# Second column parts of a feed-forward unit that stream one more tile of columns in their matmuls

## The chip, the core and the metric

The kernel runs on one NeuronCore of one Trainium2 chip. The metric is the device time of one execution in microseconds; the time before is the median of three runs. The profile is one further execution, recorded by the hardware profiler, with a time of its own.

## The reference

One decoder layer for a prompt of 2048 positions and a group of 8 x 4 sample positions that share the weights: RMSNorm, one input projection, dilated attention and a gated unit, output projection, then a SwiGLU feed-forward part, a residual add and a final RMSNorm. All in float32. The part that the change touches is the feed-forward:

```python
def _swiglu(x, g, w_gate, w_up, w_down):
    h = _rmsnorm(x, g)
    return (jax.nn.silu(h @ w_gate) * (h @ w_up)) @ w_down
# D_MODEL = 1024, D_FF = 2816
```

## The kernel before

The first thousand microseconds hold the projections and the attention; the rest is output projection and feed-forward, which go through the prompt in three blocks: `Block(0, 6)`, `Block(6, 12)` and `Block(12, NT)`, tiles of 128 rows. Blocks 0 and 1 have six tiles, the last one four, plus the sample rows, whose columns are dealt out to its tiles.

The two products with w_gate and w_up are computed together by a scheme of seven products instead of eight (Strassen's, in Winograd's form) over halves of the rows and of the inner dimension. So the feed-forward runs in units: one unit is one of the 22 columns of 128 hidden features (`f`), for all tiles of a block, in seven products `q = 0..6`. `product` (L1651) makes one of them: four slices of the inner dimension, and for each three matmuls (L1661 to L1663), since every float32 operand is split into a high and a low part in the faster format fp32r, and high x high, high x low and low x high are summed in PSUM. That is 12 matmuls a product, 84 a unit. The weight part (`op`, 128x128 slices) is the stationary operand; the block's normalised input (`xh2`, `xl2`, made by `Operands`, L1464) is the moving one, with a width of `B.w` columns for each tile: 64 in blocks 0 and 1, 68 in the last one. A whole unit streams 6 x 64 = 384 or 4 x 68 = 272 columns in each matmul.

`ps_m` (L87) hands out four PSUM banks in turn. After the matmuls ACT copies the first product out (L1671), DVE adds the others up (L1673 to L1690), ACT applies silu (L1701), and `hidden` (L1704) multiplies and splits the result into `hw`, high part by ACT (L1711), low part by DVE one step later (through `later` and `tick`, L1316 to L1324). Every second unit, `down_unit` (L1719, matmuls L1734) multiplies two units' results by w_down, in two halves for each tile, into two PSUM banks in turn, and DVE adds them to `acc` (L1736).

The stationary operands of unit f + 1 are prepared while unit f runs (`prepare`, L1625, from `one`, L1991): ACT rounds (`high`, L1600), GpSimd subtracts (`low_half`, L1604). In block 0 they are also made there from the weights for the first time, ACT scaling them by the norm's gain (L1572) and GpSimd forming the scheme's four sums (`sums`, L1584 to L1593), and are then stored to `ab_d`; blocks 1 and 2 load them from there. The rows of w_down are split by ACT and GpSimd as well (`split_down`, L1647, by `split_sb` at L135 and L138). Each engine works through its instructions in the order in which the program issues them, written out by hand.

The first unit of each block (f = 0) is cut in two column parts, so that it can begin while the last tiles' operands are still being made: `part = 4 if B.nt == 6 else 2`, and

```python
units = [dict(f=0, a=0, b=part), dict(f=0, a=part, b=B.nt)] + [dict(f=f, a=0, b=B.nt) for f in range(1, NF)]
```

So in blocks 0 and 1 the first part streams tiles 0 to 3 (256 columns) and the second one tiles 4 and 5 (128 columns); in the last block both stream two tiles (136 columns). During the second part the operands of unit 1 are prepared (L2002), as beside any other unit.

Of the kernel before, what the change touches and what calls it, by code (L numbers as in the profile page):

```python
# [65 lines left out]
def hymba_step(ctx: ExitStack, tc: tile.TileContext, A: dict, O: dict):  # L66
# [20 lines left out]
    def ps_m(which=None):  # L87

        if which is None:
            turn[3] = which = (turn[3] + 1) % 4  # L90
        return pool_["pm"].tile([P, 512], F32, name="ps_m%d" % which, tag="m%d" % which, bufs=1)
# [610 lines left out]
    for half in range(2):  # L702
        for ki, kind in enumerate(ORDER[half]):
            for gi, tiles in enumerate(GROUPS):
                start = ((half * 5 + ki) * 3 + gi) * 8
                for k in range(KD):
                    if start == 0:

                        for j in range(3):
                            n = 3 * k + j  # L710
# [7 lines left out]
                for j, tj in enumerate(tiles):  # L718
# [7 lines left out]
                    ps = lambda key=key, j=j: outs[key][j]  # L726
# [459 lines left out]
    def weights_of(d, steps, n0=0, n1=NT):  # L1186
        w = {}
        at(*steps[0], lambda: w.update(w=Weights(d["s"], n0, n1)))
        for (y, ph), fn in zip(steps, "weights_a weights_b weights_c weights_d weights_e turn store".split()):
            at(y, ph, lambda fn=fn: getattr(w["w"], fn)())  # L1190
        return w

    def steps_of(s0, *steps):
        return [(s0 + y, ph) for y, ph in steps]

    last_half = {}
    for h in range(H):
# [4 lines left out]
        if end:  # L1202

            x = s0 - NI
            d = stats_of(h, dve, steps_of(x, (11, "misc"), (13, "early"), (14, "early")))
            w = weights_of(d, steps_of(x, (14, "misc"), (15, "early"), *[(15, "misc")] * 3), 0, NT // 2)
# [24 lines left out]
    for i, it in enumerate(items):  # L1231
        x, h, n = B0 + i, it["h"], it["n"]
# [47 lines left out]
    TOK = (0, 4, 1, 3, 5, 2, 6)  # L1280
# [9 lines left out]
    def wide_pair(name):  # L1290

        t_ = rp.tile([P, 2, 1024], F32R, name=name, tag="wide", bufs=2)
        return t_[:, 0], t_[:, 1]
# [22 lines left out]
    def later(n, fn, *args, ahead=False):  # L1316
        due[clock[0] + n, not ahead, len(seq)] = (fn, args)
        seq.append(0)
# [332 lines left out]
    def product(B, u, q):  # L1651

        f, a, b = u["f"], u["a"], u["b"]
        n = (b - a) * B.w
        ps = ps_m()[:, 0:n]
        wh, wl = ops[f, q]
        xh, xl = (x[:, a:b, TOK[q]] for x in B.ops)
        out = ps.rearrange("p (i w) -> p i w", w=B.w)
        for k in range(4):
            ks = slice(k * P, (k + 1) * P)  # L1660
            pe.matmul(out, wh[:, ks], xh[:, :, k], start=(k == 0), stop=False)  # L1661
            pe.matmul(out, wh[:, ks], xl[:, :, k], start=False, stop=False)  # L1662
            pe.matmul(out, wl[:, ks], xh[:, :, k], start=False, stop=(k == 3))  # L1663

        rings = ((raw_tile, raw_tile, raw_tile, zn_tile), (zn_tile, zn_tile, zn_tile, raw_tile), (zn_tile, raw_tile, zn_tile, raw_tile))[min(u["n"], 2)]
        if q in (0, 1, 3, 4):
            v = (0, 1, None, 2, 3)[q]
            u["t", v] = rings[v]()[:, 0:n]
        c11, c21, c12, c22 = (u.get(("t", v)) for v in range(4))
        if q == 0:  # L1670
            act.activation(c11, ps, AF.Copy)  # L1671
        elif q == 1:
            dve.tensor_add(c21, c11, ps)  # L1673
        elif q == 2:
            dve.tensor_add(c11, c11, ps)
            u["g", 0] = silu_of(u, 0, c11)
        elif q == 3:
            dve.tensor_add(c12, c21, ps)
            u["s1"] = ps
        elif q == 4:  # L1680
            dve.tensor_add(c21, c21, ps)
            dve.tensor_add(c22, c21, u["s1"])  # L1682
        elif q == 5:
            dve.tensor_add(c12, c12, ps)  # L1684
            u["g", 1] = silu_of(u, 1, c12)
        elif q == 6:
            if a == 0:
                B.h[f % FC] = wide_pair("hw") + (hs4[:, f // FC % 2 * FC + f % FC] if B.last else None,)
            lows = hidden(B, u, 1, c22)
            dve.tensor_add(c21, c21, ps)  # L1690
            lows += hidden(B, u, 0, c21)
            for args in lows:
                if f + 1 < NF:
                    later(1, dve.tensor_sub, *args)
                else:
                    dve.tensor_sub(*args)

    def silu_of(u, z, c):

        g = bank(z)[:, 0:c.shape[-1]] if u["f"] else c  # L1700
        act.activation(g, c, AF.Silu)  # L1701
        return g

    def hidden(B, u, zz, c):  # L1704

        f, a, b, g = u["f"], u["a"], u["b"], u["g", zz]
        dve.tensor_mul(g, g, c)  # L1707
        hh, hl, hs_ = B.h[f % FC]
        g = g.rearrange("p (i w) -> p i w", w=B.w)
        hi, lo_ = (v[:, a * P:b * P].rearrange("p (i z c) -> p i z c", z=2, c=64)[:, :, zz] for v in (hh, hl))  # L1710
        act.activation(hi, g[:, :, 0:64], AF.Copy)  # L1711
        lows = [(lo_, g[:, :, 0:64], hi.bitcast(F32))]
        if B.last:
            hi, lo_ = (hs_[:, v * SR:(v + 1) * SR].rearrange("p (z i c) -> p z i c", z=2, i=B.nt)[:, zz, a:b] for v in range(2))
            act.activation(hi, g[:, :, 64:], AF.Copy)
            lows.append((lo_, g[:, :, 64:], hi.bitcast(F32)))
        return lows
# [66 lines left out]
    B = blocks[0]  # L1784
# [192 lines left out]
    for bi, B in enumerate(blocks):  # L1977
# [13 lines left out]
        def one(u, q):  # L1991
            tick()
            product(B, u, q)
            f = u["f"]
            if u["b"] < B.nt:
# [173 lines left out]
```

## Time and profile before

| what | value |
|---|---|
| median of 3 runs | 2611.22 us (2607.18 to 2616.19) |
| the profiled execution: its own time | 2606.15 us |
| its span, first to last instruction | 2604.4 us |
| mean granted TensorE clock | 0.979 |
| TensorE, matmuls | 2484.0 us busy, 95% |
| DVE, ACT, GpSimd | 54%, 47%, 53% busy |
| matmuls of `product`, lines L1661 to L1663 | 3 x 1932, 618 us each line |
| matmuls of `down_unit`, line L1734 | 2040 of 128x512, 484 us |

How to read it: a group's line has the source line, the engine and operation, out<-in by the program's names, the shape (128x384 is partitions x streamed columns) and the count; then busy time and the mean duration of one in ns; then the idle time of the engine just before them, and who ended it. Matmuls are pipelined: the duration of one is longer than the distance from one start to the next, so costs are read from distances of starts. PE is TensorE, POOL is GpSimd; the granted clock is a share of full speed.

### The profile page before, as it was taken

The numbers are of one execution on the slowest core, as the hardware profiler recorded it, in microseconds if no ns is written. First come the engines' busy times: TensorE is split into PE (matmuls) and PEld (weight loads), VectorE is DVE, ScalarE is ACT, GpSimd is POOL, SyncE is SP. The second block draws the span as 40 slices with busy tenths as digits, with TensorE's granted clock in tenths as the row PEclk, the third lists the DMA queues.
The fourth block names the chain that finished last, engine by engine and source line by source line (L and its number), as shares of the span: only waits on it lengthen the run. The fifth ranks groups of instructions, "written<-read, shape, count | busy, mean of one in ns | idle before, by whom it ended". The sixth has DMA issues, their size and how long they took to land. (4 is left out here: it accounts for less than half of the span.)

```text
span 2604.4 us, 38948 instructions
## 1 busy us (share of the span) xinstructions
PE 2484.0 (95%) x13598; PEld 2192.0 (84%) x13598; DVE 1411.0 (54%) x2772; ACT 1220.7 (47%) x2567; POOL 1373.8 (53%) x1074
## 2 busy tenths in 40 slices
PE   8998899999999889999999999999999999999997
PEld 6777687677988777988989988999999987999996
DVE  3359686345888856444444465444444466444445
ACT  6423334446877746554554545332323335444332
POOL 2035754123576656775766743563544534666663
PEclk9999999999999999999999999999999998999998
DMA  7764853578687664464553564464554643555553
GB/s 244 223 204 146 279 152 126 180 249 271 185 231 222 170 191 159 154 201 143 177 183 129 195 184 144 170 208 156 174 186 147 209 156 118 206 197 199 198 196 110
DMA packets 313408, 479.99 MB, mean 184 GB/s; under 512 B 25841, under 2 KB 178834, under 8 KB 307326
## 3 DMA queue, kind: packets, MB, share of 16 engines
q1 hardware_dynamic: 307740, 468.48, 55.9%
q10 hardware_dynamic: 5474, 9.04, 1.2%
q8 instruction: 108, 1.77, 0.3%
q14 instruction: 86, 0.70, 0.1%
HBM read 381.72 MB, written 165.83 MB: 210 GB/s over the span
## 5 line engine op out<-in xcount | busy, mean ns | idle before, releaser
L1604 POOL TENSOR_TENSOR op<-fr,op 128x512 fp32r<-128x512 f32 x385 | 488.7, 1299 | 299.1 <-ACT op L1600 279.1
L1661 PE MATMUL ps_m<-xh,op 128*128 128x384 f32 (+4 forms) x1932 | 618.6, 320 | 3.7 <-DVE zn L1682 3.7
L1663 PE MATMUL ps_m<-xh,op 128*128 128x384 f32 (+4 forms) x1932 | 618.1, 320 | 0.0
L1662 PE MATMUL ps_m<-xl,op 128*128 128x384 f32 (+4 forms) x1932 | 617.2, 319 | 0.0
L1734 PE MATMUL ps_o<-dw,hw 128*128 128x512 f32 x2040 | 484.0, 392 | 13.1 <-DVE acc L1736 13.1
L1734 PEld LDWEIGHTS ps_o<-dw,hw 128*128 128x128 f32 x2040 | 379.6, 188 | 95.9 <-DVE acc L1736 19.8
L1661 PEld LDWEIGHTS ps_m<-xh,op 128*128 128x128 f32 x1932 | 371.8, 192 | 8.3 <-issue 2.7
L1662 PEld LDWEIGHTS ps_m<-xl,op 128*128 128x128 f32 x1932 | 371.6, 192 | 3.5
L1663 PEld LDWEIGHTS ps_m<-xh,op 128*128 128x128 f32 x1932 | 371.6, 192 | 0.0
L1736 DVE TENSOR_TENSOR acc<-acc,ps_o 128x512 f32<-128x512 f32 (+1 forms) x362 | 247.1, 687 | 213.7 <-PE ps_o L1734 213.7
L1701 ACT ACTIVATE ps_t<-zn 128x384 f32<-128x384 f32 (+1 forms) x126 | 58.3, 463 | 474.0 <-DVE zn L1684 367.8
L1600 ACT ACTIVATE op<-fr 128x512 fp32r<-128x512 f32 x396 | 235.3, 623 | 22.2 <-DMA fr<-ab_d 14.9
L138 POOL TENSOR_TENSOR dw<-fd,dw 128x1024 fp32r<-128x1024 f32 x66 | 158.7, 2405 | 122.1 <-ACT dw L135 122.1
L318 PE MATMUL ps_s<-wh,xh 128*128 128x512 f32 x480 | 197.9, 412 | 6.5 <-ACT xh L135 5.9
L319 PE MATMUL ps_s<-wl,xh 128*128 128x512 f32 x480 | 192.4, 401 | 1.0 <-DVE wl L226 1.0
L320 PE MATMUL ps_s<-wh,xl 128*128 128x512 f32 x480 | 191.6, 399 | 0.0
L1604 POOL TENSOR_TENSOR op<-pair,op 128x512 fp32r<-128x512 f32 x63 | 81.5, 1302 | 117.1 <-ACT op L1600 117.1
L1711 ACT ACTIVATE hw<-ps_t 128x384 fp32r<-128x384 f32 (+1 forms) x126 | 56.0, 453 | 175.3 <-DVE ps_t L1707 174.4
L318 PEld LDWEIGHTS ps_s<-wh,xh 128*128 128x128 f32 x480 | 93.0, 194 | 36.4 <-issue 8.3
L320 PEld LDWEIGHTS ps_s<-wh,xl 128*128 128x128 f32 x480 | 92.8, 193 | 20.6 <-DVE xl L138 0.3
L319 PEld LDWEIGHTS ps_s<-wl,xh 128*128 128x128 f32 x480 | 93.1, 194 | 19.7 <-DVE wl L226 2.2
L611 POOL TENSOR_TENSOR vl<-kv,vh 100x512 fp32r<-100x512 f32 (+1 forms) x32 | 46.0, 1438 | 109.9 <-ACT vh L605 43.9
(484 smaller groups left out, 4776.1 us busy)
## 6 DMA issues: line engine op xcount, KB each, us to landing
fr<-ab_d SPq DMA_DIRECT2D x308, 256.0 KB
fd<-in_w_down_dram SPq DMA_DIRECT2D x66, 512.0 KB
out_ks_dram<-in_cache_k_dram SPq DMA_DIRECT2D x56, 512.0 KB
out_vs_dram<-in_cache_v_dram SPq DMA_DIRECT2D x56, 512.0 KB
ab_d<-fr SPq DMA_DIRECT2D x88, 256.0 KB
raw<-in_w_in_dram SPq DMA_DIRECT2D x72, 256.0 KB
qk_d<-pair SPq DMA_DIRECT2D x64, 256.0 KB
ab_d<-pair SPq DMA_DIRECT2D x63, 256.0 KB
```

The lines of the kernel that those rows point to most:

```text
L138: (eng_lo or pool).tensor_sub(lo, src, hi.bitcast(F32))
L318: pe.matmul(o[j], xh[:, k, :], wh, start=(k == 0), stop=False)
L319: pe.matmul(o[j], xh[:, k, :], wl, start=False, stop=False)
L320: pe.matmul(o[j], xl[:, k, :], wh, start=False, stop=(k == KD - 1))
L1600: act.activation(ops[f, j][0], ab[f][j], AF.Copy)
L1604: (pool if f or j in POOL_LOW else dve).tensor_sub(lo_, ab[f][j], hi.bitcast(F32))
L1661: pe.matmul(out, wh[:, ks], xh[:, :, k], start=(k == 0), stop=False)
L1662: pe.matmul(out, wh[:, ks], xl[:, :, k], start=False, stop=False)
L1663: pe.matmul(out, wl[:, ks], xh[:, :, k], start=False, stop=(k == 3))
L1701: act.activation(g, c, AF.Silu)
L1734: pe.matmul(ps[0:nr], l_, r_[:, cs], start=(z == 0 and y == 0), stop=(z == FC - 1 and y == len(pairs) - 1))
L1736: dve.tensor_add(B.acc[i][0:nr, cs], B.acc[i][0:nr, cs], ps[0:nr])
```

## The change

In `product`, a part that doesn't begin at tile 0 takes the tile in front of it along: `lead` is 1 for the second part of a block's first unit, and 0 for all other units. The matmuls' moving operand starts one tile earlier and their output is wider by `B.w` columns: 192 in blocks 0 and 1, 204 in the last block. The rest of the code uses `ps`, which leaves the additional columns at the front of the PSUM tile out; nobody reads them. They repeat products that the first part has made for that tile.

```diff
         f, a, b = u["f"], u["a"], u["b"]
         n = (b - a) * B.w
-        ps = ps_m()[:, 0:n]
+        lead = 1 if a else 0
+        whole = ps_m()[:, 0:n + lead * B.w]
+        ps = whole[:, lead * B.w:]
         wh, wl = ops[f, q]
-        xh, xl = (x[:, a:b, TOK[q]] for x in B.ops)
-        out = ps.rearrange("p (i w) -> p i w", w=B.w)
+        xh, xl = (x[:, a - lead:b, TOK[q]] for x in B.ops)
+        out = whole.rearrange("p (i w) -> p i w", w=B.w)
         for k in range(4):
             ks = slice(k * P, (k + 1) * P)
             pe.matmul(out, wh[:, ks], xh[:, :, k], start=(k == 0), stop=False)
```

## The prediction

> **What bounds the kernel now.** I read the page first, then the clock on a fine grid, then TensorE's own rows around the three places where a block's first unit is cut in two.
>
> ```profile
> PE 2484.0 (95%) x13598; PEld 2192.0 (84%) x13598; DVE 1411.0 (54%) x2772; ACT 1220.7 (47%) x2567; POOL 1373.8 (53%) x1074
> PEclk9999999999999999999999999999999998999998
> L1661 PE MATMUL ps_m<-xh,op 128*128 128x384 f32 (+4 forms) x1932 | 618.6, 320 | 3.7 <-DVE zn L1682 3.7
> ```
>
> TensorE is busy 95% of the span, and its granted clock is not always full. So a change of TensorE's pace counts, wherever the operands keep up. The windows view, in steps of 3.413 us (columns: stretch, length, PE busy with its instructions, granted clock, DMA share, GB/s), shows the clock around the cut units:
>
> ```profile
> 1029.71:1033.12 3.41, 2.28 (x21) 1.00 0.03 10
> 1033.12:1036.53 3.41, 3.41 (x19) 0.50 0.58 219
> 1046.77:1050.19 3.42, 3.42 (x12) 0.50 0.21 77
> 1050.19:1053.60 3.41, 3.41 (x22) 1.00 0.02 5
> 1630.47:1633.88 3.41, 2.23 (x20) 1.00 0.00 0
> 1633.88:1637.29 3.41, 3.41 (x33) 1.00 0.00 0
> 2162.94:2166.35 3.41, 2.84 (x8) 0.50 0.94 355
> 2200.48:2203.89 3.41, 2.05 (x20) 1.00 0.00 0
> 2217.54:2220.96 3.42, 3.42 (x17) 0.50 0.06 21
> 2220.96:2224.37 3.41, 3.41 (x17) 0.50 0.24 78
> 2224.37:2227.78 3.41, 3.41 (x29) 1.00 0.49 150
> ```
>
> Block 0 runs at half clock from 1033.1 to 1050.2, block 2 from 2203.9 to 2224.4, and block 1 not at all. Both stretches are whole numbers of these windows (five and six). TensorE's timeline says what ran there (start, duration, engine, line, tile, shape, idle time before):
>
> ```profile
> 1019.03 0.28 PE L1662 MATMUL ps_m<-xl,op 128*128 128x256 f32 x1
> 1019.15 0.28 PE L1663 MATMUL ps_m<-xh,op 128*128 128x256 f32 x1
> 1029.37 0.28 PE L1663 MATMUL ps_m<-xh,op 128*128 128x256 f32 x1
> 1030.84 0.30 PE L1661 MATMUL ps_m<-xh,op 128*128 128x128 f32 x1 [1.19 <-DVE zn L1682]
> 1046.71 0.63 PE L1661 MATMUL ps_m<-xh,op 128*128 128x384 f32 x1
> 1047.14 0.52 PE L1662 MATMUL ps_m<-xl,op 128*128 128x384 f32 x1
> 1047.46 0.52 PE L1663 MATMUL ps_m<-xh,op 128*128 128x384 f32 x1
> 1632.79 0.30 PE L1661 MATMUL ps_m<-xh,op 128*128 128x128 f32 x1 [1.18 <-DVE zn L1682]
> 1642.19 0.39 PE L1661 MATMUL ps_m<-xh,op 128*128 128x384 f32 x1
> 2201.11 0.27 PE L1663 MATMUL ps_m<-xh,op 128*128 128x136 f32 x1
> 2202.74 0.30 PE L1661 MATMUL ps_m<-xh,op 128*128 128x136 f32 x1 [1.36 <-DVE zn L1682]
> 2218.80 0.41 PE L1663 MATMUL ps_m<-xh,op 128*128 128x136 f32 x1
> 2219.01 0.41 PE L1661 MATMUL ps_m<-xh,op 128*128 128x136 f32 x1
> 2219.65 0.53 PE L1661 MATMUL ps_m<-xh,op 128*128 128x272 f32 x1
> 2224.46 0.29 PE L1661 MATMUL ps_m<-xh,op 128*128 128x272 f32 x1
> 2238.46 5.65 PE L1734 MATMUL ps_o<-dw,hw 128*128 128x512 f32 x24
> ```
>
> The second part has 7 products of 12 matmuls, 84 in all. At full clock (block 1) they take 1642.19 - 1632.79 = 9.40 us, 111.9 ns each. At half clock they take 15.87 us in block 0 and 16.91 us in block 2.
>
> **Why the clock falls there.** At half clock 384 columns follow each other in 0.32 us, so a column streams in 0.833 ns, and in half of that, 0.417 ns, at full clock. By that, 128 columns stream 53 ns out of 111.9, that is 48% of the time. I add up the streaming time in a window. Block 0's window before the fall has the 1.19 us of idle time and some 20 narrow matmuls: 1.1 of 3.41 us, 32%, and the clock falls. Block 1's has 8 starts of 256 columns and 10 of 128: 41%, and it stays. Block 2's has about 17 of 136 columns: 28%, and it falls. A window of narrow matmuls alone (x33) is at 48% and stays. So the border lies between 32 and 41%, and block 1 escaped only by where the window's edge lay. Narrow matmuls then keep the clock down: at half clock they are 106.7 of some 213 ns (2218.80 to 2219.01), 50%. Block 2's window at 2217.54, with its last narrow matmuls and the first wide ones, is at about 68% and isn't enough; the one at 2162.94 (six 512-column streams and a piece of another) has about 78% and is. So the clock comes back between 68 and 78%.
>
> **The change part by part.** No instruction is added, removed or moved: the 252 matmuls of the second parts (3 blocks x 84) stream one tile more, 192 instead of 128 columns in blocks 0 and 1, 204 instead of 136 in block 2. The extra columns are operands that the first part has read already, so no new wait arises. They land in the part of the same PSUM tile that nobody reads, and the readers on ACT and DVE keep their sizes.
>
> Cost of the columns at full clock: no row shows 192 or 204. The nearest rows are 128 (111.9 ns) and 256 (1019.03 to 1019.15, 120 ns): 0 to 8 ns, 0 to 0.7 us for a part. Streaming 192 columns takes 80 ns of the 111.9, so I take 0. At half clock they stream in 160 and 170 ns. There, 136 columns ran at 0.21 us (2218.80 to 2219.01; 213 ns in the mean), and 272 columns take 4.81 us for 21 (2219.65 to 2224.46), 229 ns: bounds 0 to 16 ns, 0 to 1.3 us a part; again I take 0, since 170 is under 213. The Trainium skill, "TensorE: Matmul & The Clock Gate", section "Back-to-back issue gap", speaks against this: its warm gap of N/2.4 + 2.5 ns grows with every column, 27 ns from 128 to 192, 2.2 us for 84. By that, the parts would cost 6.8 us in all; but its 56 ns at N = 128 is half of this trace's 111.9.
>
> Effect on the clock: the streaming share at full clock rises to 80/111.9 = 71% (block 2: 76%), at half clock to 75% (80%). Worst window in blocks 0 and 1: 1.36 us without streaming (from 1029.37 + 0.107 to 1030.84), the rest at 71%: 43%, above the border, so no fall at any phase. Block 2's gap is 1.57 us (from 2201.11 + 0.057 to 2202.74) between 136-column matmuls of part one (51%) and the new ones: 27% if the window ends at the gap, 41% if it starts there. So it can still fall there, in about half of the phases; but then 80% brings the clock back after one window, which costs 16 matmuls x 101 ns = 1.6 us.
>
> Block 2's gain: 84 matmuls in 9.40 instead of 16.91 us, 7.5 us; then 21 matmuls of 272 columns at 229 ns instead of 126 (eleven products of 12 stand between 2219.65 and 2238.46; the 111 matmuls after 2224.46 take 14.0 us), 2.2 us. Together **9.7 us**, or 8.1 with the one window. It should reach the end, since from 2204 on TensorE waited for another engine once:
>
> ```profile
> PE ps_o L1734 <- DVE acc L1736: 1.7, 1, 1.7
> ```
>
> Block 0's gain in TensorE is 15.87 - 9.40 = 6.5 us, and 1.6 us of the next product at half clock, 8.1 us. But here GpSimd makes the operands, and it is late:
>
> ```profile
> POOL op L1604 <- ACT op L1600: 4.1, 3, 1.8
> 1033.85 2.91 DVE L1324 TENSOR_TENSOR hw<-raw,hw 128x256 fp32r<-128x256 f32 x2
> 1044.71 0.31 ACT L1701 ACTIVATE zn<-zn 128x128 f32<-128x128 f32 x1 [0.80 <-DVE zn L1684]
> 1052.14 2.40 POOL L138 TENSOR_TENSOR dw<-fd,dw 128x1024 fp32r<-128x1024 f32 x1
> 1071.27 5.64 PE L1734 MATMUL ps_o<-dw,hw 128*128 128x512 f32 x24
> 1099.01 2.40 POOL L138 TENSOR_TENSOR dw<-fd,dw 128x1024 fp32r<-128x1024 f32 x1
> 1120.62 3.02 PE L1734 MATMUL ps_o<-dw,hw 128*128 128x512 f32 x12 [0.78 <-DVE acc L1736]
> ```
>
> In the pair of units after, the third half of the down projection starts at 1120.62, after a wait, 21.6 us behind GpSimd's split at 1099.01. The chain is GpSimd, then ACT's copies behind it in its queue, then DVE's evacuations. In block 0's first pair the split is at 1052.14, so that chain allows the third half at 1073.75, and TensorE gets to it at 1071.27 + 2.7 = 1074.0 (two halves of 12 matmuls take 5.64 with the last one's tail): it is 0.25 us from waiting already. So block 0 gains 0.25 us and what GpSimd gains, no more. GpSimd idled 4.1 us between 1030 and 1056 (first row), for ACT. Only ACT's 0.80 us wait at 1044.71 came from TensorE's slow products; an earlier one stands behind DVE's 2.91 us subtraction, which the change doesn't touch. So the gain is 1.0 us (bounds 0.25 and 4.4, and 8.1 if the chain is no chain), and some 7 us of TensorE's lead turn into waits before 1073. If over 2.1 us of that wait falls into one window, the window is under the border and the clock falls there: one window at half clock, -1.7 us. I take **0** for block 0 (bounds -3 and 8). Block 1 ran at full clock: 0 (bounds -0.7 and 0).
>
> Sum: 2606.15 - 9.7 = 2596.5 us on the profiled execution's own time (span 2604.4). That execution was 5.1 us below the median of the runs, 2611.22 (2607.18 to 2616.19). Some of these 5.1 us may be block 1's part at half clock in other executions (about 8 us each time), which would go too; the rest stays. So the median after lies between 2596.5 and 2601.6, and I take the middle, **2599**.
>
> **Rivals.** First, block 0 gives its 8.1 us as well: if the chain at 1073 follows TensorE rather than GpSimd: 2596.5 - 8.1 = 2588.4 to 2593.5. Against it stand the 21.6 us above.
>
> Second, the clock doesn't follow the streamed columns, and the change doesn't do what it can do: every second part behaves as before, 2606 to 2611. The same skill page, section "Why this matters for your kernels", asks only for no idle gaps over about 3 us; by that rule the 1.2 to 1.4 us gaps here wouldn't trip the gate, with or without wider streams. The trace disagrees: it fell right behind them. What speaks against this rival is that block 1, with the same gap, kept its clock.
>
> Third, slower: the clock falls as before, isn't brought back by 75 to 80%, and the wide matmuls cost at half clock what 272 columns do. Place: the second parts of blocks 0 and 2; price 84 x 16 ns = 1.3 us each, and 0.7 us in block 1 at full clock: +3.3, 2609 to 2614.5. It decides from the point where the half-clock restart needs more than 80%; the window at 2162.94 (78%) speaks against.
>
> Fourth, columns are paid for from the first one on: 64 x 0.417 = 27 ns a matmul, 2.2 us in block 1 and 2.4 in block 2, hidden in block 0: 2601 to 2606. The 136-column parts of block 2, no slower than 128 columns at half clock (213 ns), speak against.
>
> **How the numbers follow.** Forecast (block 2 gains, block 0 doesn't; 2593 to 2605) 0.65; block 0 too 0.10; no effect 0.12; slower 0.08; paid columns 0.05. The range 2591 to 2608 holds the forecast, the fourth rival, about half of the first and some of the second. A measurement of this kernel can tell about 0.3%, 7.8 us, from no change, so faster means below 2603.4. That has 0.60 of the forecast, 0.10 and 0.02: 0.72. Slower by that much is only the third's tail, 0.03. The rest, 0.25, is within.
>
> **What would show it.** Right: in block 2 the 84 matmuls of the second part take 9.4 us (11 with one window at half clock), at 112 ns; the clock row shows no 17 and 20 us stretches; in block 0 TensorE waits about 7 us more between 1040 and 1075 for operands, accumulators or DVE. Wrong: half clock all through a second part (the gate looks at something else), spacing near 120 or 140 ns (columns cost), or the third half of block 0's first down projection 5 us or more earlier than before.

## The result: 13.7 us less, and the profile after

The median went from 2609.39 us (six runs, 2605.74 to 2616.19) to 2595.71 us (six runs, 2590.91 to 2601.38). The ratio of the runs is 0.9943 with a 95% interval of 0.9924 to 0.9962; that of the two medians is 0.9948. The profiled execution after took 2590.91 us (span 2589.1), 15.2 less than the one before. From the page of the changed kernel, the busy line and the clock row:

```profile
PE 2463.9 (95%) x13598; PEld 2173.8 (84%) x13598; DVE 1413.7 (55%) x2772; ACT 1221.1 (47%) x2567; POOL 1376.7 (53%) x1074
PEclk9999999999999999999999999999999999999998
```

The 8 of before in the slice from 2148.6 to 2213.7 us is gone; the 8 of the last slice stays. Block 0's half clock never showed in this row: its 17.1 us lay in two slices, and both still read 9. (The matmul lines of `product` are L1663 to L1665 now, those of the down projection L1736.) The windows on the clock's grid, whose edges lie elsewhere in each execution (stretch, length, PE busy with its instructions, granted clock, DMA share, GB/s):

```profile
1021.17:1024.58 3.41, 2.21 (x20) 1.00 0.02 5
1024.58:1028.00 3.42, 3.42 (x33) 1.00 0.42 153
1062.14:1065.55 3.41, 0.59 (x3) 1.00 1.00 285
1065.55:1068.97 3.42, 3.42 (x10) 0.50 0.82 266
1068.97:1072.38 3.41, 3.41 (x19) 1.00 0.74 270
1208.90:1212.31 3.41, 3.41 (x9) 0.50 0.97 317
2195.36:2198.77 3.41, 2.06 (x19) 1.00 0.00 0
2198.77:2202.18 3.41, 3.41 (x33) 1.00 0.06 17
```

The first row and the last but one are the windows with the idle gap ahead of a second part. TensorE is busy in them for about as long as before (2.21 and 2.06 us, against 2.28 and 2.05), yet the window behind each stays at 1.00: with the wider matmuls, the streams fill 44 and 45% of them, where it was 32 and 28%. Two half-clock windows are new. The one at 1065.55 follows a window in which TensorE was busy for 0.59 us: the lead that block 0's part gained had turned into waiting. The one at 1208.90 lies further on in block 0. TensorE's timeline after has the ends of the second parts and these waits:

```profile
2196.72 0.33 PE L1663 MATMUL ps_m<-xh,op 128*128 128x204 f32 x1 [1.35 <-DVE zn L1684]
2206.16 0.31 PE L1663 MATMUL ps_m<-xh,op 128*128 128x272 f32 x1
1047.08 0.44 PE L1665 MATMUL ps_m<-xh,op 128*128 128x384 f32 x1 [1.68 <-POOL op L1604]
1059.42 2.59 PE L1736 MATMUL ps_o<-dw,hw 128*128 128x512 f32 x9 [1.29 <-ACT hw L1713]
1064.96 4.61 PE L1736 MATMUL ps_o<-dw,hw 128*128 128x512 f32 x12 [2.95 <-DVE acc L1738]
```

Block 2's part takes 2206.16 - 2196.72 = 9.44 us, 16.91 before. In block 0, 5.9 us of waits stand in three places ahead of the down projection's third half (a half is six matmuls, so the third begins with the thirteenth, at 1064.96).

To compare executions that differ elsewhere, I read from each timeline the stretch of a block: first product of its first part to first product of its unit 3.

| kernel | block 0 | block 1 | block 2 | half clock in these stretches |
|---|---|---|---|---|
| before | 75.6 | 67.5 | 64.8 | 17.1 in block 0's second part, 20.5 in block 2's |
| after | 76.1 | 67.5 | 55.2 | 3.4 in block 0, at the down projection |

So the change itself gave 9.6 us in block 2, took 0.5 in block 0, and gave nothing in block 1. These 9.1 us are not all of the 15.2 between the two profiled executions: 7.9 us arose ahead of the first changed instruction, and 1.8 were lost between and behind the stretches (0.6 of them in the rest of block 0, where the fall at 1208.90 is). Block 0's first product starts at 1018.5 us before and at 1010.6 after, with the same instructions up to there. Over the ten other profiled executions below it lay between 1013.97 and 1020.66. That is the noise of one execution; the medians carry less of it.

### The profile page after: what moved, and what is told of

Same layout as the page of the kernel before. It is cut to its first block, busy times and chain, and to the rows that moved or that the text cites. A ratio compares the mean times of both kernels' runs of the same rounds, so it can differ in the third digit from the quotient of the medians.

```text
span 2589.1 us, 38948 instructions
## 1 busy us (share of the span) xinstructions
PE 2463.9 (95%) x13598; PEld 2173.8 (84%) x13598; DVE 1413.7 (55%) x2772; ACT 1221.1 (47%) x2567; POOL 1376.7 (53%) x1074
## 3 DMA queue, kind: packets, MB, share of 16 engines
q1 hardware_dynamic: 307740, 468.48, 56.8%
## 5 line engine op out<-in xcount | busy, mean ns | idle before, releaser
L1663 PE MATMUL ps_m<-xh,op 128*128 128x384 f32 (+5 forms) x1932 | 611.1, 316 | 3.7 <-DVE zn L1684 3.7
L1665 PE MATMUL ps_m<-xh,op 128*128 128x384 f32 (+5 forms) x1932 | 610.9, 316 | 1.7 <-POOL op L1604 1.7
L1664 PE MATMUL ps_m<-xl,op 128*128 128x384 f32 (+5 forms) x1932 | 609.9, 316 | 0.0
L1736 PE MATMUL ps_o<-dw,hw 128*128 128x512 f32 x2040 | 487.8, 394 | 16.5 <-DVE acc L1738 15.2
L1736 PEld LDWEIGHTS ps_o<-dw,hw 128*128 128x128 f32 x2040 | 381.7, 189 | 100.7 <-DVE acc L1738 22.3
L1663 PEld LDWEIGHTS ps_m<-xh,op 128*128 128x128 f32 x1932 | 364.2, 189 | 8.3 <-issue 2.7
L1664 PEld LDWEIGHTS ps_m<-xl,op 128*128 128x128 f32 x1932 | 363.9, 188 | 3.5
L1665 PEld LDWEIGHTS ps_m<-xh,op 128*128 128x128 f32 x1932 | 363.8, 188 | 2.0 <-POOL op L1604 2.0
L320 PEld LDWEIGHTS ps_s<-wh,xl 128*128 128x128 f32 x480 | 92.3, 192 | 20.5 <-DVE xl L138 0.3
```

The lines of the kernel that those rows point to most:

```text
L320: pe.matmul(o[j], xl[:, k, :], wh, start=False, stop=(k == KD - 1))
L1736: pe.matmul(ps[0:nr], l_, r_[:, cs], start=(z == 0 and y == 0), stop=(z == FC - 1 and y == len(pairs) - 1))
```

## The experiments

Theory A is the prediction's: the clock falls after a window of 3.413 us in which streamed columns fill less than a border between 32 and 41%, and comes back after one that is filled to 68 to 78% or more; and block 0 is held by GpSimd's queue. Each kernel is told as an edit of the one before or the changed one. Where a kernel was run once, its verdict rests on the stretches of its profile, not on its total.

### Without the gap, narrow and wide

```diff
-        ps = ps_m()[:, 0:n]
+        ps = (ps_o() if a and q == 0 else ps_m())[:, 0:n]
```

The second part's first product goes to a bank of the other ring, and the wait for DVE's read of the bank (L1682) is gone. The wide kernel has the same edit in `whole`. A wait of 0.6 us for DVE later in block 0's second part stays in both.

> The kernel before, narrow second parts (128 and 136 columns), but the second part's first product goes into a PSUM bank of the ring that the output projection has left, so that it doesn't wait for DVE's read of the first part's fourth product, and the 1.2 to 1.4 us gap goes. Measured are the stretches from a block's first product to the first product of its unit 3: before 75.6, 67.5, 64.8 us in blocks 0, 1, 2; after 76.1, 67.5, 55.2. Theory A (the gate falls when the streamed columns fill less than 32 to 41% of a window): narrow matmuls alone fill 48 to 51%, so no fall: block 2 in 53.8 (55.2 less the gap), block 1 in 66.3, block 0 within 1 us of before; total about 2593. Theory B (narrow matmuls are what the gate falls on, and only the wider stream holds it): block 2 falls as before, 63.4; total about 2606.

> The changed kernel with the same other PSUM bank for the second part's first product, so wide and without the gap. Theory A: block 2 in 53.8, block 1 in 66.3, block 0 the same as after within 1.5 us (GpSimd sets its end); total 2.6 us under the change, the same as the narrow kernel without the gap. Theory B: the same 53.8 here, and 10 us less than the narrow one.

Measured: narrow 76.1, 66.1 and 53.8 us, wide 74.5, 66.1 and 53.8. Medians 2592.31 both (ten runs each; ratios to before 0.9941, interval 0.9923 to 0.9960, and 0.9938, 0.9919 to 0.9958), so the totals don't tell these two kernels apart. The windows of the narrow kernel, with nothing but 128 or 136 columns in the second, third and fifth row:

```profile
1023.04:1026.45 3.41, 3.41 (x31) 1.00 0.02 5
1026.45:1029.86 3.41, 3.41 (x33) 1.00 0.00 0
1627.20:1630.61 3.41, 3.41 (x33) 1.00 0.00 0
2193.81:2197.22 3.41, 3.40 (x31) 1.00 0.00 0
2197.22:2200.63 3.41, 3.41 (x31) 1.00 0.00 0
```

Narrow matmuls without the gap keep the full clock, as theory A has it; theory B (63.4 in block 2) is out. The extra columns are not needed for their own sake: they make up in the window for the gap's idle time. Block 0's 76.1 and 74.5 differ by a fall at the first down projection, which the narrow kernel had and the wide one not.

### The change in some blocks only

```diff
-        lead = 1 if a else 0
+        lead = 1 if a and B.last else 0
```

The other kernel has `not B.last`.

> The change in the last block alone (204 columns there, 128 in blocks 0 and 1). Theory A, with GpSimd as block 0's limit: the whole gain is here. Block 2 in 55.2, or 56.8 with one window at half clock; block 0 in 75 to 76.5 whether or not its clock falls; block 1 in 67.5, or 75 if its window falls badly. If block 0's part gave something in the changed kernel, its stretch is shorter there than here by up to 8 us.

> The change in blocks 0 and 1 alone (192 columns there, 136 in the last block). Theory A: block 2 falls in most phases of the window, 64.8 (55.2 in about one of six); block 0 in 75 to 76.5 without a fall in its second part, block 1 in 67.5.

Measured: last block alone 76.1, 75.5 and 56.8 us (2603.09 in all); first blocks alone 76.1, 67.5 and 64.8 (2607.35). The first of these executions shows by chance what the others hide. Its windows in block 1, narrow, and block 2, wide:

```profile
1628.58:1631.99 3.41, 2.43 (x22) 1.00 0.00 0
1631.99:1635.40 3.41, 3.41 (x18) 0.50 0.05 8
2205.43:2208.84 3.41, 2.06 (x18) 1.00 0.00 0
2208.84:2212.25 3.41, 3.41 (x19) 0.50 0.00 0
2212.25:2215.67 3.42, 3.42 (x32) 1.00 0.81 268
```

In block 1 the narrow part fell (the streams fill 34% of the window ahead) and stayed at half clock for 17.1 us: block 1 can lose 8.0 us, 75.5 against 67.5, and before merely hadn't in the profiled execution. In block 2 the wide part fell too (35%), and was back after one window; the stretch is 1.6 us longer than 55.2, as the prediction priced it. And block 0 took 76.1 with a narrow part at full clock as with a wide one.

### A longer gap

```diff
             dve.tensor_add(c21, c21, ps)
+            for _ in range(8 * (u["b"] < B.nt)):
+                dve.tensor_scalar(c21, c21, 1.0, None, op0=OP.mult)
             dve.tensor_add(c22, c21, u["s1"])
```

> The changed kernel with the gap in front of the second part made 2.4 to 3.5 us longer (eight multiplications by 1 on DVE between the two additions after the first part's fifth product), so that the clock falls there in every phase and every block. Theory A with the restart border between 68 and 78%: 192 and 204 columns fill 75 and 80% at half clock, so the clock is back after one or two windows, and the second part takes 11 to 12.8 us in blocks 1 and 2. The rival with the border above 80%: half clock through the whole part, 17.9 us.

> The kernel before with the same longer gap. Theory A: 128 and 136 columns fill 50 and 53% at half clock, under the border, so every second part that falls stays at half clock to its end: 15.5 to 17.9 us in blocks 1 and 2, and block 2's stretch some 8 us longer than in the wide kernel with the long gap. The rival with the border above 80%: as long in both kernels.

Measured: the gap grew by 3.2 and 2.9 us in blocks 1 and 2, as meant, but by 6.2 us in block 0. The second parts take 12.4, 12.5 and 11.4 us in the wide kernel, and 17.95, 17.95 and 17.96 in the narrow one; block 2's stretch 60.1 and 68.2. First the wide kernel's windows in block 1, then the narrow one's (the first two and the last of its six at half clock, and the next one):

```profile
1642.85:1646.27 3.42, 0.00 (x0) 1.00 0.00 0
1646.27:1649.68 3.41, 3.09 (x15) 0.50 0.00 0
1649.68:1653.09 3.41, 3.41 (x18) 0.50 0.01 4
1653.09:1656.50 3.41, 3.41 (x32) 1.00 0.85 301
```

```profile
1640.50:1643.91 3.41, 3.08 (x15) 0.50 0.00 0
1643.91:1647.33 3.42, 3.42 (x18) 0.50 0.14 20
...
1657.57:1660.98 3.41, 3.41 (x14) 0.50 0.27 71
1660.98:1664.39 3.41, 3.41 (x22) 1.00 0.04 16
```

The matmul count of a half-clock window is the same, 18, and a start follows the one before in 213 ns in both kernels: at half clock the wider stream costs nothing. But 192 columns fill 75% of it and the clock is back; the window ahead, 66% filled, was not enough. 128 columns fill 50%, and the clock waits for the wide matmuls of unit 1. So the wide stream does two things: it makes the fall rarer, and it ends it early. The rival with a border above 80% is out.

### Two tiles in front

```diff
-        lead = 1 if a else 0
+        lead = 2 if a else 0
```

> The changed kernel with two tiles in front streamed along (256 columns in blocks 0 and 1, 272 in the last). If columns are free until streaming reaches the 112 ns floor and then cost as the wide rows: 120 and 126 ns a matmul, second parts of 10.1, 10.1 and 10.6 us (9.4 in the changed kernel), block 2's stretch 56.4, and no fall in any phase. If each column is paid for from the first: the same here, but then 192 would have cost 116 or more, which the changed kernel's 111.8 has not.

Measured: 10.1 us for the second parts of blocks 0 and 1 (84 x 120.7 ns), block 2's part 12.2 and its stretch 57.9 (10.6 and 56.4 expected), with one window at half clock; total 2595.93. The columns' price is as expected. "No fall in any phase" was wrong: the window ahead of the fall held 1.0 us of the first part's 136 columns, the gap and 0.9 us of wide matmuls, 36%. Wider streams cannot help in the part of a window that lies ahead of the gap.

### What holds block 0

```diff
-                split_down(f)
+                split_down(f, dve if bi == 0 and f == 0 else None)
```

`split_down` hands the engine on to `split_sb`. The two kernels after it have no gap, narrow parts, and `f < 2` or no condition on f, at both calls.

> The changed kernel with the low half of block 0's first w_down row computed by DVE instead of GpSimd (one 128x1024 subtraction, 2.4 us on GpSimd, which DVE does between two evacuations). Theory A, GpSimd's queue sets when block 0's first down projection goes on: the split is ready earlier, the second w_down row can be loaded earlier, and all that stands behind comes 2.4 us or more earlier. Block 0's stretch 73.7 or less without a fall (76.1 in the changed kernel, 74.4 without its fall), and less waiting on ACT and DVE ahead of the third half. If TensorE's own path or the DMA of the second row sets it, the stretch stays at 74.4 to 76.1.

Measured: 74.7 us in block 0, with a fall of one window as in the changed kernel's 76.1, so 1.4 us gained and not 2.4. By itself, 74.7 would also fit the other expectation, 74.4 to 76.1; what speaks for GpSimd is the gain between two kernels that both have the fall, and where it arose. GpSimd's sum beside DVE's subtraction took 2.15 us instead of 1.30, and its queue ran on without a pause behind it. The second w_down row was split 1.4 us earlier against the block's second part (27.6 us after its start, 29.0 in the changed kernel), and the third half of the down projection came 1.4 us earlier. So the queue is the limit, and its relief was less than the instruction's length.

> The narrow kernel without the gap, with the low halves of block 0's first two w_down rows on DVE: GpSimd is relieved of 2 x 2.4 us in the run of subtractions behind block 0's cut unit. One such row on DVE gained 1.4 us of block 0's stretch there (76.1 to 74.7, both with the clock's fall at the first down projection). If GpSimd's queue is still the limit, two give about 3 to 4: block 0 in 72.5 to 73, or 71 to 71.5 without the fall. If DVE or ACT has become the limit, no shorter than 74.5. Blocks 1 and 2 as without the gap, 66.1 and 53.8.

> The same with the low halves of all of block 0's w_down rows on DVE. TensorE waits 0.8 us or more for the accumulators ahead of the third half of each pair of units in block 0 (5.6 us in five pairs before), behind GpSimd's queue and ACT's. If GpSimd's 2.4 us count in each pair, these waits go, and block 0's remainder (unit 3 to block 1's first product, 526.4 us before, 524.8 without the gap) becomes 6 to 9 us shorter; total about 2581. If ACT's scaling or the evacuations set them, it stays at 524 to 526.

Measured: with two rows on DVE block 0 takes 71.7 us without a fall, against 74.5 (wide, no gap, no fall): 2.9 us gained, a little less than expected. The total is 2591.03 us, ratio 0.9925, interval 0.9901 to 0.9949, which doesn't tell it from the kernel without the gap alone. With all of block 0's rows on DVE the remainder of block 0 takes 514.1 us, 10.6 less than without the gap alone (524.8) and more than the 6 to 9 expected, and the total is **2574.6 us** (four runs, 2570.97 to 2576.37; some 2581 expected), ratio 0.9869, interval 0.9833 to 0.9904: better than before and than the change. What TensorE and ACT waited for in block 0's remainder (us in total, times, longest), first in the kernel before (1094 to 1614 us), then in this one (1088 to 1602 us):

```profile
PE ps_o L1734 <- DVE acc L1736: 10.4, 12, 2.2
ACT op L1600 <- POOL pair L1593: 32.8, 9, 4.9
ACT dw L135 <- DMA fd<-in_w_down_dram: 30.5, 10, 3.9
```

```profile
PE ps_o L1734 <- DVE acc L1736: 1.3, 3, 0.7
ACT op L1600 <- POOL pair L1593: 4.7, 9, 1.5
ACT dw L135 <- DMA fd<-in_w_down_dram: 5.1, 10, 0.6
```

The releaser that TensorE's rows name is DVE, but the work that was taken away was GpSimd's. DVE's additions stand behind evacuations that wait for ACT, and ACT waited for GpSimd's sums: a wait's row names only the last link. ACT's wait for the landing of the w_down rows shrank as well; which of ACT's two waits counted was not separated. Without the gap alone, TensorE's wait was still 9.2 us, so removing the gap is not what shortened it.

## Why the prediction was right

- **The clock's border.** Held. Windows ahead of a second part were followed by half clock at 34, 35 and 36%, beside the 32 and 28% of before, and by full clock at 41% and above. Counted in the same way over all full-clock windows of the twelve traces that hold nothing but matmuls of `product` and the down projection, the border is narrower: up to 39.0% half clock followed (change in the first blocks alone, at 1213.2), from 39.1% full clock (two rows on DVE, at 1035.0). The streams decide, and not how long TensorE is busy: a window with 1.80 us busy at 512 columns (41%; wide kernel without the gap, at 1063.59) kept the clock, and one with 2.77 us busy at 128 columns (36%; shown at the end) lost it. The Trainium skill, "TensorE: Matmul & The Clock Gate", section "Why this matters for your kernels", puts the danger at idle gaps over about 3 us; here 1.2 us were enough among narrow matmuls. The restart border is between 68% (not enough in the kernel before) and 75% (enough for 192 columns). The count of columns is not the whole measure everywhere. In the attention part, with transposes among the matmuls, two half-clock windows came back at 56 and 64% by the same count, while in the changed kernel one at 321.4 us, ahead of the attention, did not at 77%. In the output projection a window with 34% kept the clock (change in the last block alone, at 969.8) where one with 37% lost it (two tiles in front, at 970.9). What else counts there was not tried.
- **The price of the columns.** Zero held. The second parts take 9.43, 9.43 and 9.44 us at full clock with 192, 192 and 204 columns (9.40 with 128). So the rival that pays for each column from the first one is out (11.6 us by its working).
- **Block 2.** 9.7 forecast, 9.6 measured in the stretch; and 8.0 with a fall at the gap, 8.1 forecast. Of the three profiled executions with 204 columns and the usual gap, two had that fall; the forecast put it at about half.
- **Block 0.** Its part fell from 15.87 to 9.43 us, and nothing came of it, as forecast. The third half follows the first split of w_down by 1064.96 - 1043.42 = 21.5 us (21.6 in the forecast); against the block's first product it came 1.2 us earlier than before, and the waits ahead of it were 5.9 us, about 7 in the forecast. They caused one fall. The two terms that the prediction had for this, 1.0 us gained and 1.7 lost, give 0.7 lost together; 0.5 was measured, and 0 had been taken. In the wide kernel without the gap, where the fall didn't come, the stretch is 1.0 us shorter than before. The stretch is 76.1 in five kernels with the fall, narrow or wide, with the gap or not, with one tile more or two.
- **Block 1.** Right for the profiled executions. That it can lose 8 us in others was put down as a part of the median's distance from the profile; the kernel with the change in the last block alone showed the loss once. How often it occurs in unprofiled runs stays open.
- **The total.** 2599 was the middle of 2596.5 and 2601.6; 2595.7 lies just below both. The measured difference of the medians, 13.7 us, is more than the 9.1 us that the stretches give, and the interval of the ratio (9.9 to 19.8 us) starts above them. The rest can be block 1's falls, chance, or both, and no run here tells these apart. So the parts were forecast from their causes, but that the total came so close is partly luck.

The chain that the point on block 0 speaks of, in the changed kernel's timeline, from GpSimd's split and the sum behind it in its queue, for which ACT waits, over ACT's and DVE's evacuations to the additions that free the accumulators (GpSimd has no pause between the first two rows, ACT none between its two):

```profile
1043.42 2.39 POOL L138 TENSOR_TENSOR dw<-fd,dw 128x1024 fp32r<-128x1024 f32 x1
1054.33 1.28 POOL L1593 TENSOR_TENSOR pair<-fr,pair 128x512 f32<-128x512 f32 x1
1055.65 0.63 ACT L1600 ACTIVATE op<-pair 128x512 fp32r<-128x512 f32 x1 [3.55 <-POOL pair L1593]
1062.13 0.47 ACT L1673 ACTIVATE zn<-ps_m 128x384 f32<-128x384 f32 x1
1062.63 0.56 DVE L1675 TENSOR_TENSOR raw<-zn,ps_m 128x384 f32<-128x384 f32 x1 [2.58 <-ACT zn L1673]
1064.23 1.28 DVE L1738 TENSOR_TENSOR acc<-acc,ps_o 128x512 f32<-128x512 f32 x2
```

## What to carry to other kernels

Where matmuls are short against the distance of their starts, add up the streamed columns per clock window: a gap of a microsecond between narrow matmuls can halve the clock for as long as the matmuls stay narrow. Removing the gap does as much for the clock as streaming more, and saves the gap as well (block 2: 53.8 against 55.2 us). Before counting a faster stage as a gain, look for the queue that feeds the stages behind it: here the same 8 us were worth all in one block and nothing in another.

## What was not expected of the hardware

A kernel without the gap still fell once. With all of block 0's rows on DVE, TensorE waited 0.6 us for DVE in the narrow second part; the streams filled that window to 36% only, and the two windows behind it ran at half clock:

```profile
1031.59:1035.00 3.41, 2.77 (x26) 1.00 0.41 154
1035.00:1038.41 3.41, 3.41 (x19) 0.50 0.02 6
1038.41:1041.83 3.42, 3.42 (x14) 0.50 0.38 141
1041.83:1045.24 3.41, 3.41 (x21) 1.00 0.25 88
```

It cost nothing there: block 0 took 71.7 us, as in the kernel with two rows on DVE, which had the same wait across the edge of two windows, filled to 39 and 49%, and kept its clock. Narrow matmuls at 48% have little room above the border, and that is what the wider stream still buys. The other surprise is the size of chance: the same instructions up to block 0's first product took between 1010.6 and 1020.7 us, and the clock's windows lie differently over the same instructions in each execution, which alone decides on a fall near the border (block 1's narrow part with the gap: 41% and no fall before, 34% and a fall with the change in the last block alone).
